# Another order of the parts, three small results on GpSimd, and a last tile in three groups of heads, in a hybrid attention and state-space layer

## The chip, the cores and the metric

One core of one Trainium2 chip runs the whole layer. The metric is device time in microseconds for one execution. Of three runs of the kernel before, the median was 692.42 us (692.40 to 692.64). The engines are TensorE (PE, with its weight loads as PEld), VectorE (DVE), ScalarE (ACT), GpSimd (POOL) and SyncE (SP), which here only issues transfers (DMAs). Each engine works through its own queue in order; semaphores make it wait for other engines and for transfers.

## What is computed

The input x has 1024 tokens of width 1024, in float32, one layer, one sequence. The reference, cut to what matters:

```python
mod = silu(c) @ w_ada + b_ada                       # shift, scale, gate
h = rms_norm(x, norm_g) * (1 + scale) + shift
q, kcr, vcr, ksl, vsl, kwn, vwn, z_a, g_br, u, z_s = split(h @ w_in)
kc, vc = rms_norm(compress(kcr)), compress(vcr)     # 63 blocks of 32 tokens
attn = g0 * softmax(q kc) vc + g1 * softmax(rq rk_slc, chosen blocks) v_slc
     + g2 * softmax(rq rk_win, last 512 tokens) v_win
attn = attn * silu(z_a)                             # 8 heads of 64, 2 key groups
y = gelu(s5(u)); y = y * sigmoid(y @ glu_w + glu_b) # complex diagonal recurrence
mix = concat(attn, y * silu(z_s)) @ w_out
return x + gate * mix
```

`s5` is a recurrence over the 1024 tokens with 32 groups of 16 channels and 64 complex states each.

## The kernel before, in words

The tokens are cut into 8 tiles of 128. The kernel keeps float32 accuracy by splitting an operand into a high and a low part (`hhi`, `hlo`; `wh`, `wl`; `oh`, `ol`) and adding three matmul products. High parts are casts on ACT, low parts a subtraction on DVE, on GpSimd, or an accumulating transfer.

The stages, in the order of time:

- x is loaded; its squares are summed (`sq`, in x_squares), the columns of `w_ada` are multiplied with silu(c) and summed (`wada`, in mod_chunk, a DVE product of 128x1024 for each 128 columns), and h is formed, transposed and split. A step named h`k``n` forms chunk k of half n.
- Projections of h go to keys and values (`kk`, normed, then `ropeb` is a rotary product and `kr` the rotated sum on GpSimd), to the S5 input (`U`), and to the raw keys and values of the compressed branch. A weight slice is loaded (`wr`, `wraw`), cast on ACT (`wh`, `wsp`) and its low part subtracted (`wl`, `wsp`).
- S5 runs in four scans of 8 groups each. For scan s, `prep` builds matrices from the parameters (tiles ta, tb, tc_, td, `s5W`, `s5CA`), `tables` the turning factors (`s5tab`), `mats` the kernel `Kt`, stored into `s5T` by eight transfers; `U` is stored to DRAM (`ud`) and loaded in another layout by eight transfers (`s5X`). Then `scan` takes `pvv` (PE), copies it to `zw` (four ACT copies), turns it with six DVE products (`z`, `zw`), scans it twice (tensor_tensor_scan) and turns it back; `out` computes `py` from `s5X` and the resulting `z`, copies it to `Y` and stores it (`yd`) through GpSimd's queue.
- Compressed keys, the gates z (pieces z0_0 to z7_7), and the GLU (`pglu`, `tg`, `zz` loaded again, `ps`) follow. The heads of the attention run through five steps: ha (scores `S`, row maxima `st`, exponentials `pp`), hs (reciprocals), hb and hc (weights `hl` in float16, transposed by transfers from SP into `PT`), ub (products `po`). While a score tile waits for its exponential, PE cannot fill it again.
- The output projection: `so` for the S5 half, `wo` for weights, `at` and `ao` for the attention half of a tile (unit_b, attn_trans, attn_out, out_half), with the last tile handled by last_out.

What sets the order is the table `ORD` (lines 27 to 56): names of parts, run in the order of the table, each of which adds its instructions to the queues; the framework's scheduler may then put an instruction behind one that is ready earlier on the same engine. `FLG` (line 57) says which engine does a small operation (d for DVE, p for GpSimd, a for ACT, t for an accumulating transfer). Nearly all transfers are issued by SP, in order: a store that waits for its data holds back every load behind it. The lines of the profile that the steps touch: 140 (dma), 148 (scalar_tensor_tensor) and 151 (tensor_tensor), which are helpers, 208 (cast of weights), 826 (`zw` copies), 853 (`py` from `z`), 1187 (row maxima), 1306 (out_half) and 1320 (last_out).

The part that releases the last tile:

```python
    def out_half(i, n, p):
        r = M["ps"][:, i, halves(n)]
        o = f2([128, 512], F32, "o")
        tt(dve, o[:], p[:], M["gate"][:, halves(n)], OP.mult)
        on = FLG.get(f"ao{i}{n}", "d")
        if on == "t":
            pool.dma_start(o[:], r, accum_op=OP.add)
        else:
            tt({"p": pool, "d": dve}[on], o[:], o[:], r, OP.add)
        dma(out.rearrange("(a p) d -> p a d", p=128)[:, i, halves(n)], o[:], "O")
```

Of the kernel before, what the change touches and what calls it, by code (L numbers as in the profile page):

```python
# [1619 lines left out]
```

## Time and profile before

| | |
|---|---|
| median of 3 runs | 692.42 us |
| the profiled execution | 691.38 us |
| its span, first to last instruction | 689.5 us |
| PE busy | 623.5 us, 90% |
| DVE busy | 567.3 us, 82% |
| ACT busy | 377.9 us, 55% |
| GpSimd busy | 148.6 us, 22% |
| mean granted clock of TensorE | 0.98 |
| mean DMA rate over the span | 169 GB/s |

The profiled execution is one run; its span lies 1.88 us under its own time, and its time 1.04 us under the median. Busy shares are means over stages that differ, so a stage is read from its own timeline: which engine stands still, until when, and what it was given at that moment. In a timeline, an entry with "x2" or more joins equal instructions that follow each other, and its duration is that of the group; the square brackets hold the idle time before it and what ended it.

### The profile page before, as it was taken

The page shows a single profiled execution, that of the slowest core. Times are in us where ns is not written, and L with a number is a line of the kernel's source. Part 1 is how long each engine was busy: PE and PEld are TensorE (multiplying, and loading weights), DVE is VectorE, ACT ScalarE, POOL GpSimd, SP SyncE. Part 2 cuts the span into 40 slices and gives each one's busy share as a digit, 9 for nine tenths or more (in the row PEclk, how much of TensorE's full clock was granted, in tenths as well). Part 3 has the DMA queues.
Part 4 walks back from the last instruction along what each step waited for, and adds up shares of the span by engine and source line. Part 5 has one row for each costly group of instructions (what it writes and reads, how often), then busy time and mean ns, then how long its engine had stood idle before and what let it go on. Part 6 is the DMA issues. An engine that isn't in the chain of part 4 may idle for free.

```text
span 689.5 us, 12618 instructions
## 1 busy us (share of the span) xinstructions
PE 623.5 (90%) x4662; PEld 492.1 (71%) x4662; DVE 567.3 (82%) x1106; ACT 377.9 (55%) x732; POOL 148.6 (22%) x159
## 2 busy tenths in 40 slices
PE   2478999999698999999999999989899999799996
PEld 0356787788587886888788887556677777687775
DVE  5998999777937889876677787998898998998872
ACT  3677413735162252555586786547756855756640
POOL 0153209147232020640011101132001220011010
PEclk9989999999899999999999999999999999999999
DMA  8975211355276624373656868499689599688994
GB/s 319 417 246 104 47 62 41 115 158 136 64 246 199 212 68 109 83 231 94 131 139 154 207 186 183 124 207 208 183 172 206 132 226 222 184 215 213 224 222 86
DMA packets 209759, 116.76 MB, mean 169 GB/s; under 512 B 159073, under 2 KB 188513, under 8 KB 209698
## 3 DMA queue, kind: packets, MB, share of 16 engines
q1 hardware_dynamic: 205858, 109.38, 61.5%
q0 software_dynamic: 3840, 6.57, 4.0%
q8 instruction: 37, 0.61, 0.3%
q14 instruction: 24, 0.20, 0.1%
HBM read 58.10 MB, written 18.61 MB: 111 GB/s over the span
## 4 chain that ended last, share of the span: by engine, by line
PE 41%; DVE 21%; issue 5%; ACT 4%; DMA 2%; SPq 1%; POOL 1%; DVEq 0%; ACTq 0%; POOLq 0%
PE pcp L351 9%; PE po L1053 8%; PE S L1170 7%; DVE hl L148 4%; PE po L1263 3%; PE pglu L1015 3%; DVE st L1187 3%; PE ptp L331 2%; PE ptp L332 2%; PE ptp L330 1%; DVE ps L151 1%; ACT pp L1203 1%; DVE z L151 1%; PE pg L530 1%; PE ph L901 1%
## 5 line engine op out<-in xcount | busy, mean ns | idle before, releaser
L1203 ACT ACTIVATE pp<-S,st 128x640 f32<-128x640 f32 (+7 forms) x128 | 88.6, 699 | 60.5 <-DVE st L1187 46.5
L148 DVE SCALAR_TENSOR_TENSOR hl<-pp,st,hl 128x640 f16<-128x640 f32 (+7 forms) x128 | 100.5, 817 | 4.9 <-ACT hl L1222 4.8
L1222 ACT ACTIVATE hl<-pp,st 128x640 f16<-128x640 f32 (+7 forms) x128 | 85.2, 728 | 8.2 <-DVE st L151 7.1
L1053 PE MATMUL po<-wo,oh 128*128 128x512 f32 x264 | 85.2, 407 | 3.7 <-DVE wo L151 2.4
L351 PE MATMUL pcp<-hhi,wh 128*128 128x512 f32 x208 | 84.8, 408 | 0.0
L351 PE MATMUL pcp<-hhi,wl 128*128 128x512 f32 x208 | 82.6, 397 | 0.0
L351 PE MATMUL pcp<-hlo,wh 128*128 128x512 f32 x208 | 82.4, 396 | 0.0
L1187 DVE TENSOR_REDUCE st<-S 128x1 f32<-128x1024 f32 (+3 forms) x64 | 57.5, 916 | 6.9 <-PE S L1170 6.7
L1170 PE MATMUL S<-kT,qh 128*128 128x128 f32 (+3 forms) x192 | 60.7, 375 | 1.0 <-ACT pp L1203 0.7
L1053 PEld LDWEIGHTS po<-wo,oh 128*128 128x128 f32 x264 | 48.7, 191 | 14.9 <-DVE wo L151 3.8
L330 PE MATMUL ptp<-wsp,hhi 128*128 128x512 f32 x128 | 53.5, 420 | 6.5 <-ACT hhi L296 4.1
L1263 PE MATMUL po<-V,PT 128*128 128x64 f16 x1584 | 59.0, 193 | 0.0
L1263 PEld LDWEIGHTS <-PT 128*128 128x128 f16 x1584 | 54.0, 98 | 5.7 <-issue 5.1
L1170 PE MATMUL S<-kT,ql 128*128 128x128 f32 (+3 forms) x192 | 55.3, 346 | 0.1
L332 PE MATMUL ptp<-wsp,hlo 128*128 128x512 f32 x128 | 53.0, 416 | 1.5 <-POOL hlo L151 1.5
L331 PE MATMUL ptp<-wsp,hhi 128*128 128x512 f32 x128 | 53.5, 418 | 0.5 <-DVE wsp L151 0.5
L151 POOL TENSOR_TENSOR qr<-ropeb 128x512 f32<-128x512 f32 x16 | 23.5, 1488 | 121.7 <-DVE ropeb L151 69.7
L1053 PE MATMUL po<-wo,ol 128*128 128x512 f32 x120 | 47.9, 402 | 0.8 <-DVE ol L151 0.8
L1170 PEld LDWEIGHTS S<-kT,qh 128*128 128x128 f32 x192 | 33.7, 193 | 17.2 <-issue 11.8
L351 PEld LDWEIGHTS pcp<-hlo,wh 128*128 128x128 f32 x208 | 39.1, 188 | 9.2
L351 PEld LDWEIGHTS pcp<-hhi,wh 128*128 128x128 f32 x208 | 39.2, 189 | 8.3
L351 PEld LDWEIGHTS pcp<-hhi,wl 128*128 128x128 f32 x208 | 39.2, 188 | 8.1
(327 smaller groups left out, 1351.5 us busy)
## 6 DMA issues: line engine op xcount, KB each, us to landing
wada<-in_w_adaT_dram SPq DMA_DIRECT2D x24, 512.0 KB, 6.6
wr<-in_w_in_dram SPq DMA_DIRECT2D x14, 512.0 KB, 4.5
x<-in_x_dram SPq DMA_DIRECT2D x8, 512.0 KB, 6.8
wor<-in_w_out_dram SPq DMA_DIRECT2D x8, 512.0 KB, 4.5
out_dram<-o SPq DMA_DIRECT2D x16, 256.0 KB, 2.5
wraw<-in_w_in_dram SPq DMA_DIRECT2D x15, 256.0 KB, 4.7
xo<-in_x_dram SPq DMA_DIRECT2D x14, 256.0 KB, 3.4
ud<-U SPq DMA_DIRECT2D x4, 512.0 KB, 3.2
```

The lines of the kernel that those rows point to most:

```text
L148: dve.scalar_tensor_tensor(out=o, in0=a, scalar=s, in1=b, op0=o0, op1=o1, **kw)
L151: e.tensor_tensor(out=o, in0=a, in1=b, op=op)
L330: pe.matmul(p, H(k)[:, tsl], w[:, 0, :], start=k == 0, stop=False)
L331: pe.matmul(p, H(k)[:, tsl], w[:, 1, :], start=False, stop=False)
L332: pe.matmul(p, H(k, True)[:, tsl], w[:, 0, :], start=False, stop=k == 7)
L351: pe.matmul(p[:], w[:, k, :], H(k, l)[:, halves(half)], start=(k == 0 and w is hi and not l), stop=(k == 7 and l))
L1053: pe.matmul(p, a[x][:, k, :], w[y][:, halves(n)], start=k == 0 and m == 0, stop=k == 3 and m == 2)
L1170: pe.matmul(R[:, c0:c1], w, x, start=bank not in opened, stop=False, skip_group_check=True)
L1187: dve.tensor_reduce(out=st[br], in_=us[br][0][:, :W], axis=AX.X, op=OP.max, negate=True)
L1203: act.activation(pp[:, :W], R[:, :W], AF.Exp, bias=st[br], accum_out=st4[:, 1, 2 * (h % 2) + br:2 * (h % 2) + br + 1])
L1222: act.activation(hl[:, :W], pp[:, :W], AF.Copy, scale=st[br])
L1263: pe.matmul(o, p, v, start=first, stop=end, skip_group_check=True)
```

## The change

A fifth of the names in `ORD` stand elsewhere, most of them by one to five places; two results move to another engine at the start (`sq2` from ACT to DVE, `h21` from DVE to GpSimd), and two adds of the output projection go from DVE to GpSimd (`ao21`, `ao40`). The last tile's attention heads 4 to 7, projected together before, are now projected as pairs: heads 4 and 5, then 6 and 7, and a new step `lo` (last_halves) ends the tile. The projection of one group is issued after the transposes (`pat`) of the next have been put behind it. A list `LATE`, empty here, has no effect. The number of matmuls is the same.

```diff
-sc1 sc0 lb pu xl_0 sq0 sq2 sq1 sq3 ma7 mb4 ma0 rstd0 mb0 kvaw0 ma5 xl_1 xsc0 sq5 xb10 sq4 xb00 sq6 sq7 mg mc0 h00 mb2
+sc1 sc0 xl_0 sq2 sq0 sq3 pu ma7 mb4 ma0 sq1 lb rstd0 mb0 ma5 kvaw0 xsc0 xl_1 xb00 sq5 xb10 sq4 sq6 sq7 mg mc0 h00 mb2
...
-cU3 mats1 kpat1 xl1 kvb7 kpb0 tq kpb1 kpbn0 u2 qaw0 u3 mod0 mod1 out0 prep2 tab1 cVC kpbn1 scan1 out1 tab2 xl2 cmpk
+cU3 mats1 xl1 kpat1 kvb7 kpb0 tq kpb1 kpbn0 u2 qaw0 u3 mod0 mod1 prep2 kpbn1 tab1 cVC out0 scan1 out1 tab2 xl2 cmpk
...
-    cw2456="d", cw512="d", cw640="d", h00="p", h01="d", h10="p", h11="t", h20="p", h21="d", h30="d", h31="d", h40="d",
+    cw2456="d", cw512="d", cw640="d", h00="p", h01="d", h10="p", h11="t", h20="p", h21="p", h30="d", h31="d", h40="d",
-    qw0="d", qw1="d", qw2="d", qw3="d", qw4="d", qw5="d", qw6="t", qw7="d", sq0="d", sq1="a", sq2="a", sq3="d",
+    qw0="d", qw1="d", qw2="d", qw3="d", qw4="d", qw5="d", qw6="t", qw7="d", sq0="d", sq1="a", sq2="d", sq3="d",
-    ao01="d", so1="d", at1="p", ao10="d", ao11="d", so2="p", at2="p", ao20="d", ao21="d", so3="d", at3="p", ao30="d",
+    ao01="d", so1="d", at1="p", ao10="d", ao11="d", so2="p", at2="p", ao20="d", ao21="p", so3="d", at3="p", ao30="d",
-    ao31="d", so4="d", ao40="d", ao41="d", so5="d", at5="p", ao50="d", ao51="d", so6="d", at6="p", ao60="d", ao61="d",
+    ao31="d", so4="d", ao40="p", ao41="d", so5="d", at5="p", ao50="d", ao51="d", so6="d", at6="p", ao60="d", ao61="d",
...
     def unit_b(i, h, br):
-        first = br == 0 and (j == 0 if last else h == 0)
+        first = br == 0 and (h in (0, 4, 6) if last else h == 0)
...
-        if br and j == 3 and (g or last):
+        if br and (h in (3, 5, 7) if last else h == 7):
...
-            hs = slice(4 * g if last else 0, 4 * g + 4)
+            hs = slice({3: 0, 5: 4, 7: 6}[h] if last else 0, h + 1)
...
-    def last_out(i, g):
-        if g == 0:
+    def last_out(i, hs):
+        if hs.start == 0:
...
+        else:
+            for n in range(2):
+                outproj(LO["p"][n][:], LO["a"], 0, n, LO["k"])
         za = LO["za"]
-        ks = (2 * g, 2 * g + 1)
-        kk = slice(2 * g, 2 * g + 2)
+        kk = slice(hs.start // 2, hs.stop // 2)
+        ks = range(kk.start, kk.stop)
+        w = 128 * len(ks)
...
         hi, lo = LO["a"]
         act.copy(hi[:, kk], za[:, kk])
         tt(dve, lo[:, kk], za[:, kk], f32(hi[:, kk]), OP.subtract)
+        LO["k"] = ks
+
+    def last_halves():
+        i = OB[-1]
         for n in range(2):
-            outproj(LO["p"][n][:], LO["a"], 0, n, ks)
-            if g:
-                out_half(i, n, LO["p"][n])
+            outproj(LO["p"][n][:], LO["a"], 0, n, LO["k"])
+            out_half(i, n, LO["p"][n])
```

What a few rows of the table do to the queues shows at three places. Lines of the changed file are one higher than before.

The first place is SP's queue between the stores of `U` for scans 2 and 3 and the X loads of scan 2. Before:

```order
68 L140 DMA ud_110<-U 128x1024
69 L140 DMA wraw<-in_w_in_dram 128x512
70 L140 DMA wada<-in_w_adaT_dram 128x1024
71 L140 DMA ud_111<-U 128x1024
72 L140 DMA wada<-in_w_adaT_dram 128x1024
73 L140 DMA wr_1560<-in_w_in_dram 128x8x128
74 L140 DMA s5X<-ud_110 16x8x128 x8
75 L140 DMA wraw<-in_w_in_dram 128x512 x2
```

and now:

```order
68 L141 DMA ud_110<-U 128x1024
69 L141 DMA wraw<-in_w_in_dram 128x512
70 L141 DMA s5X<-ud_110 16x8x128
71 L141 DMA ud_111<-U 128x1024
72 L141 DMA wada<-in_w_adaT_dram 128x1024 x2
73 L141 DMA s5X<-ud_110 16x8x128
74 L141 DMA wr_1539<-in_w_in_dram 128x8x128
75 L141 DMA s5X<-ud_110 16x8x128 x6
76 L141 DMA wraw<-in_w_in_dram 128x512 x2
```

Both `wada` loads now stand behind the second store of `U`, and ahead of `wr`; two of the eight X loads stand ahead of `wr` and six behind it.

The second place is DVE's queue between the `wada` products that go with those loads and scan 1, whose first instructions are the products that write `z`. Before:

```order
343 L151 TENSOR_TENSOR tc__1534<-s5P,s5c 128x512
344 L148 SCALAR_TENSOR_TENSOR wada,macc<-wada,sc 128x1024
345 L151 TENSOR_TENSOR td<-s5P,s5c 128x512
346 L151 TENSOR_TENSOR tb<-s5f,s5x 128x384
347 L151 TENSOR_TENSOR s5W<-tc__1534,td 128x512
348 L151 TENSOR_TENSOR s5tab<-ta,tb 128x4x96
349 L151 TENSOR_TENSOR wl_1559<-wr_1560,wh_1558 128x1024
350 L151 TENSOR_TENSOR ta<-s5f,s5x 128x384
351 L151 TENSOR_TENSOR tb<-s5f,s5x 128x384
352 L151 TENSOR_TENSOR ropeb<-kk,cs 128x512
353 L151 TENSOR_TENSOR s5tab<-ta,tb 128x4x96
354 L151 TENSOR_TENSOR ropeb<-kk,cs 128x512
```

and now:

```order
342 L152 TENSOR_TENSOR td<-s5P,s5c 128x512
343 L152 TENSOR_TENSOR tb<-s5f,s5x 128x384
344 L152 TENSOR_TENSOR s5W<-tc__1504,td 128x512
345 L816 MEMSET rho 128x4
346 L152 TENSOR_TENSOR ropeb<-kk,cs 128x512 x2
347 L149 SCALAR_TENSOR_TENSOR wada,macc<-wada,sc 128x1024
348 L152 TENSOR_TENSOR s5tab<-ta,tb 128x4x96
349 L149 SCALAR_TENSOR_TENSOR wada,macc<-wada,sc 128x1024
350 L152 TENSOR_TENSOR ta<-s5f,s5x 128x384
351 L152 TENSOR_TENSOR tb<-s5f,s5x 128x384
352 L149 SCALAR_TENSOR_TENSOR mod<-macc,bada 128x1 x2
353 L152 TENSOR_TENSOR s5tab<-ta,tb 128x4x96
```

The tc and td products, s5W and both ropeb stand ahead of the two `wada` products; before, td, tb and s5W stood behind the second one, and ropeb behind `wl`. The loads of `wada` are the ones above.

The third is the end of DVE's queue: the last tile. Before:

```order
940 L148 SCALAR_TENSOR_TENSOR za<-za,vsc,pat 128x256
941 L151 TENSOR_TENSOR oh<-za,oh 128x256
942 L148 SCALAR_TENSOR_TENSOR za<-za,vsc,pat 128x256
943 L151 TENSOR_TENSOR oh<-za,oh 128x256
944 L151 TENSOR_TENSOR o<-po,gate 128x512
945 L151 TENSOR_TENSOR o<-o,ps 128x512
946 L151 TENSOR_TENSOR o<-po,gate 128x512
947 L151 TENSOR_TENSOR o<-o,ps 128x512
```

and now:

```order
936 L149 SCALAR_TENSOR_TENSOR za<-za,vsc,pat 128x256
937 L152 TENSOR_TENSOR oh<-za,oh 128x256
938 L149 SCALAR_TENSOR_TENSOR za<-za,vsc,pat 128x128
939 L152 TENSOR_TENSOR oh<-za,oh 128x128
940 L149 SCALAR_TENSOR_TENSOR za<-za,vsc,pat 128x128
941 L152 TENSOR_TENSOR oh<-za,oh 128x128
942 L152 TENSOR_TENSOR o<-po,gate 128x512 x2
943 L152 TENSOR_TENSOR o<-o,ps 128x512
```

The second group of 256 columns became two of 128, and one of the two final adds is no longer here; it is the last operation of GpSimd's queue. In SP's queue ahead of scan 0, the store of the rotated keys (`kTd`) moved from behind the last seven X loads to in front of them. On GpSimd the two kr ahead of scan 1 now stand behind seven of the stores of `yd`.

## Rows read from the trace of the kernel before

**Rows 1.** The page, part 1: busy us, share of the span and instructions

```profile
PE 623.5 (90%) x4662; PEld 492.1 (71%) x4662; DVE 567.3 (82%) x1106; ACT 377.9 (55%) x732; POOL 148.6 (22%) x159
```

**Rows 2.** PE's waits: us in total, times, longest us

```profile
PE S L1170 <- ACT pp L1203: 10.6, 13, 3.3
PE py L853 <- DVE z L151: 6.2, 1, 6.2
...
PE ptp L330 <- ACT wsp L208: 2.4, 2, 1.9
...
PE pvv L824 <- DMA s5X<-ud: 1.2, 1, 1.2
...
PE pw L795 <- ACT Kt L785: 0.5, 1, 0.5
```

**Rows 3.** Timeline of PE; start, us, line, op, [idle before <-releaser]

```profile
184.93 0.80 PE L853 MATMUL py<-z,s5CA 128*128 128x127 f32 x2 [6.19 <-DVE z L151]
```

**Rows 4.** Timeline of DVE, 154 to 186 us

```profile
161.98 2.03 DVE L148 SCALAR_TENSOR_TENSOR wada<-wada,sc 128x1024 f32<-128x1024 f32 x1 [4.09 <-DMA wada<-in_w_adaT_dram]
...
171.94 2.37 DVE L151 TENSOR_TENSOR z<-zw,s5tab 128x512 f32<-128x512 f32 x2
174.24 1.78 DVE L151 TENSOR_TENSOR zw<-zw,s5tab 128x512 f32<-128x512 f32 x1
```

**Rows 5.** Timeline of ACT, 148 to 187 us

```profile
164.46 1.05 ACT L208 CAST wh<-wr 128x1024 fp32r<-128x1024 f32 x1 [7.61 <-DMA s5X<-ud]
...
165.93 2.38 ACT L826 COPY zw<-pvv 64x512 f32<-64x512 f32 x4
168.34 0.41 ACT L763 COPY s5tab<-s5f 128x256 f32<-128x256 f32 x1
```

**Rows 6.** Timeline of SP, 148 to 187 us: DMA issues

```profile
156.66 0.33 SPq L140 DMA_DIRECT2D ud<-U  x1
157.04 0.43 SPq L140 DMA_DIRECT2D wada<-in_w_adaT_dram  x1
157.58 0.66 SPq L140 DMA_DIRECT2D wr<-in_w_in_dram  x1
```

**Rows 7.** The tile wr, 140 to 175 us: landing of its one load

```profile
DMA to landing us min/median/max: 6.7/6.7/6.7
```

**Rows 8.** Timeline of DVE, 104 to 134 us: start of scan 0

```profile
126.75 1.30 DVE L151 TENSOR_TENSOR z<-zw,s5tab 128x512 f32<-128x512 f32 x2 [4.30 <-ACT zw L826]
127.97 0.68 DVE L151 TENSOR_TENSOR zw<-zw,s5tab 128x512 f32<-128x512 f32 x1
```

**Rows 9.** Timeline of GpSimd (POOL), 154 to 186 us

```profile
153.76 2.37 POOL L140 DMA_DIRECT2D yd<-Y  x4
...
172.02 3.46 POOL L151 TENSOR_TENSOR kr<-ropeb 128x512 f32<-128x512 f32 x2 [4.48 <-DVE mod L148]
```

**Rows 10.** Two us: busy time of PE, PEld, DVE, ACT, POOL; PEclk, DMA, GB/s

```profile
186.00:188.00 2.00, 2.00 (x11) 2.00 (x11) 1.97 (x6) 0.00 (x0) 0.00 (x0) 0.51 0.51 134
```

**Rows 11.** Timeline of DVE, 8 to 26 us

```profile
16.91 1.11 DVE L148 SCALAR_TENSOR_TENSOR rstd<-rsq,rstd 128x4 f32<-128x4 f32 x1
```

**Rows 12.** Timeline of GpSimd, 8 to 26 us

```profile
16.74 1.27 POOL L151 TENSOR_TENSOR wsp<-wraw,wsp 128x512 fp32r<-128x512 f32 x1 [15.54 <-ACT wsp L208]
```

**Rows 13.** Timeline of SP, 104 to 134 us

```profile
117.06 3.43 SPq L140 DMA_DIRECT2D s5X<-ud  x7
120.59 0.61 SPq L140 DMA_DIRECT2D kTd<-kh  x1
```

**Rows 14.** Timeline of DVE, 452 to 474 us

```profile
459.90 2.06 DVE L151 TENSOR_TENSOR ps<-tg,zz 128x512 f32<-128x512 f32 x1 [0.26 <-DMA zz<-zsd]
461.80 1.84 DVE L148 SCALAR_TENSOR_TENSOR hl<-pp,st,hl 128x640 f16<-128x640 f32 x1
```

**Rows 15.** Timeline of PE, 452 to 474 us

```profile
466.73 0.22 PE L1170 MATMUL S<-dmask,identb 128*128 128x128 bf16 x1 [3.27 <-ACT pp L1203]
```

**Rows 16.** Timeline of DVE, from 679 us to the end

```profile
685.72 0.69 DVE L151 TENSOR_TENSOR o<-o,ps 128x512 f32<-128x512 f32 x1
```

More of the change, by code (lines that the diff above doesn't have):

```diff
@@ new lines @@
+h20 xb21 h30 kvaw3 xb11 h11 h21 xb31 kvaw6 xb40 mc5 h31 ma4 s5l mc4 ll h40 xb70 mc7 h70 xb50 u0m ma6 h50 kva0 kva1
+xb51 kva2 u1m xb61 u2m u3m xb60 mc6 h51 h61 xb71 xb41 h60 kva3 tb h41 kva4 kvaw7 h71 s5p kva5 kva6 sw u4m u5m kva7 u6m
+u7m tabf kpa0 kpa1 kvb0 cKC kpan0 kvb1 kvb2 prep0 kvb3 kvb4 kvb5 u0 cU2 mats0 kpat0 tab0 kvb6 xl0 prep1 scan0 kpan1 u1
+cU3 mats1 xl1 kpat1 kvb7 kpb0 tq kpb1 kpbn0 u2 qaw0 u3 mod0 mod1 prep2 kpbn1 tab1 cVC out0 scan1 out1 tab2 xl2 cmpk
+qaw1 cmpv kpbt0 qaw2 mod2 mod3 mod4 mats2 hidk qaw3 qaw4 qaw5 qa0 qa1 qa2 kpbt1 qa3 mod5 qa4 qa5 qaw6 mod6 qaw7 qa6
@@ new lines @@
+qw2 ct1 ha12 ha13 z3_3 qr2 ub04 ub05 ha14 hs13 ub06 ha15 z3_4 z3_5 cz5 ub07 z3_6 z3_7 hs15 z4_0 hb12 hb13 ub10 hb14
+hb15 qt20 ub11 ha16 ha17 hc12 hc13 hc14 yp02 z4_1 z4_2 hs17 qt21 hb16 ub12 ha20 ha21 hb17 z4_3 ca2 hc15 hs21 ha22 z4_4
+z4_5 ha23 hc16 z4_6 z4_7 hb20 ub13 cz6 hb21 hc17 hs23 hc20 yp03 yp10 ub14 z5_0 z5_1 z5_2 hb22 z5_3 z5_4 ub15 qw3 qr3
+z5_5 hc21 cz7 z5_6 ha24 hb23 ha25 ub16 ub17 hs25 hb24 z6_0 z5_7 hc22 hc23 hc24 ha26 ha27 ct2 hs27 qt30 z6_1 z6_2 z6_3
+z6_4 z6_5 z6_6 yp11 z6_7 yp12 hb25 hb26 hc25 ha30 ha31 qt31 ha32 ha33 hs31 hs33 ca3 hb27 z7_0 hb30 ub20 hc26 hb31 z7_1
@@ new lines @@
+glul z7_2 z7_3 hb32 z7_4 hc27 z7_5 hc30 hc31 hc32 ha34 yp13 ub21 qw7 hb33 ha35 hs35 z7_6 z7_7 hc33 ct3 sp glu00 grow
+ha36 ha37 glu03 qr7 qt70 glu01 hb34 hc34 qt71 ha70 ub22 ub23 ub24 hb35 ha71 ub25 hc35 ca7 ub26 ub27 hs37 hb36 hc36
+ub30 hb37 ct7 glu11 glu02 glu12 glu10 hs71 hb70 qw6 qr6 ha72 ub31 ub32 ub33 hc37 hc70 at0 ha73 hs73 glu13 wo10 wo11
+hb71 hc71 hb72 hc72 ha74 hb73 wo12 wo13 ub34 ub35 ub36 ha75 qt60 hc73 ub37 hs75 hb74 hb75 ub70 ha76 ha77 hs77 ub71 so0
+so1 qt61 hc74 hc75 hb76 hb77 ca6 ub72 hc76 hc77 ha60 ha61 ub73 hs61 hb60 ub74 hc60 ct6 qw5 hb61 ha62 ha63 so2 hs63 qr5
@@ new lines @@
+hb62 ub75 ha64 hc61 hc62 hb63 ha65 ub76 hs65 so4 hb64 hb65 ha66 ha67 ub77 ca5 ub60 ub61 hc63 hc64 so5 qt50 ub62 ha50
+qt51 hs67 hb66 hb67 hc65 qw4 qr4 ub63 so7 hc66 ha51 hc67 hs51 ub64 hb50 hb51 hc50 hc51 so6 ha52 ha53 ha54 ha55 ha56
+ub65 hs53 hb52 hb53 ub66 so3 wo00 wo01 wo02 wo03 ct5 hc52 qt41 at3 hc53 ub67 ub50 hs55 hb54 hb55 hc54 ha57 hs57 ca4
+ao30 hc55 ao31 ao00 ao01 qt40 hb56 hb57 at1 at2 ao10 ha40 ha41 hs41 hb40 hc56 hb41 hc57 hc40 ha42 ub51 ao11 ha43 ub52
+ao20 hs43 hb42 ct4 hb43 hc41 hc42 ao21 ha44 ha45 hc43 ub53 hs45 ub54 at7 ao70 hb44 hb45 ub55 ao71 ha46 ub56 ub57 ub40
@@ L56 @@
+at5 at6 ha47 ao50 ao51 ao61 hc44 hs47 ub41 hc45 hb46 hc46 hb47 ao60 ub42 ub43 ub44 ub45 ub46 hc47 ub47 lo
 """.split()
@@ L70 @@
 SMB = 11
+LATE = []
 OA, OB = [0, 1, 2, 3], [7, 6, 5, 4]
@@ L1534, in hymba @@
     it.pop(f"at{OB[-1]}")
+    I("lo", f"ub{OB[-1]}7")(last_halves)
     for n in range(2):
```

42 lines of the change are left out of this document (11 added, 31 removed).

## The prediction

> **What bounds the kernel.** I read the busy table first. TensorE (PE) works 623.5 us of a span of 689.5 us [rows 1], and the change issues the same matmuls. So the time moves only by PE's idle time, some 66 us, or by matmuls that run at another clock. Next I read PE's waits. Three of them lie where the diff moves instructions: 6.2 us for VectorE's (DVE's) z before the first `py<-z` of scan 1, 10.6 us in 13 pieces for the exponentials that free the score tiles, and 1.2 us for the X transfer of scan 0 [rows 2]. Then I followed each wait back on the engine it names.
>
> The 6.19 us at 184.93 [rows 3] end when scan 1 ends on DVE. Its first z starts at 171.94; ahead of it DVE waited 4.09 us in its queue for a `wada` transfer (to 161.98), and the `wada` product that follows took 2.03 us [rows 4]. ScalarE (ACT) waited 7.61 us, to 164.46, then cast `wh`, and only then copied pvv into zw (from 165.93) and wrote s5tab (168.34) [rows 5]: the wait is booked to an X transfer, but the cast reads `wr`, issued at 157.58 [rows 6], which needs 6.7 us to land [rows 7], so at 164.3. Within the scan the first two z took 2.37 us and the next zw 1.78 us [rows 4], against 1.30 and 0.68 us in scan 0 [rows 8]. GpSimd's two kr ran beside them, 172.02 to 175.48 [rows 9].
>
> The clock is the last view: while PE waits it falls to half, 0.51 from 186 to 188 us [rows 10], so PE's first work after the wait, 184.93 to about 188, is done at 1.2 GHz.
>
> **The scan 1 stage (the main term).** On DVE the change puts both ropeb and the tc, td, s5W work before the `wada` products, so the 4.09 us wait is filled. On GpSimd kr now follows the first seven yd stores. GpSimd's four yd stores took 2.37 us [rows 9], so seven take about 4.1 us; the Y copies can end near 159 (U ends just before the ud store at 156.66 [rows 6]), the stores near 163, two kr of 1.73 us (half of 3.46) near 166.5. That is ahead of the scan, which then costs its clean durations. It ran from 171.94 to 184.93, 12.99 us; less 2.37 − 1.30 and 1.78 − 0.68, together 2.17 us, it takes 10.8 us.
>
> On the other side stands SyncE's (SP's) queue: both `wada` loads are now issued ahead of `wr`, with one X load. One more 512 KB goes in front of `wr`. The nearest rows give its price: the `wada` issued at 157.04 was used at 161.98, and `wr`, issued 0.54 us later, landed 2.3 us after that [rows 4, 6, 7]. So `wr` lands between 164.3 (six of the eight X loads now lie behind it) and 168.5 (the price twice); I take 167.2, the price once and 0.6 us for issues. From the landing ACT needs the cast (1.05), four zw copies (2.38) and s5tab (0.41) [rows 5]: z can start at about 171.0, and DVE's wl, 2.3 us behind the landing, is done before. The start gains 0.9 us (bounds −0.4 and 3.8, by the two ends of the landing), the scan 2.2: **−3.1 us** at the first `py`. The chain behind it (Y, yd, G copies, pk, s5T) keeps its order, and DVE and ACT shift with PE. Some is lost where a transfer's landing ends a wait that isn't released by this chain: PE waits 2.4 us in all for wsp casts of freshly loaded `wraw` [rows 2]. Between 0 and 1.9 us of the gain could be eaten there; I take 0.6. If the wait shrinks to about 3 us, PE's clock probably still falls; I count nothing there.
>
> What the Trainium skill would make of the kr overlap: its page "SBUF — State Buffer", section "SBUF: two separate sides", says that the ports that DVE and GpSimd share are locked for a whole instruction and the loser blocks fully. By that, moving kr away would free two whole GpSimd operations, 2 × 1.27 = 2.5 us instead of 2.17. The trace agrees for one small operation: a DVE rstd that began at 16.91 ended when GpSimd's wsp did, 1.11 us later [rows 11, 12].
>
> **The X transfer of scan 0.** SP now issues the 512 KB kTd store before the seven X loads instead of after them; before, the loads took 3.43 us to issue from 117.06 and the store 0.61 us from 120.59 [rows 13]. So the last X load is issued 0.61 us later, and lands between 0.6 and 1.9 us later (its transfer queued behind 512 KB, bounded by the 2.3 us price above less what drains in the 3.4 us of issuing). Against it, pk and pw go earlier on PE and save the 0.5 us wait for Kt [rows 2]. Net **+0.5 us** (−0.5 to +1.4).
>
> **The GLU stage.** PE waits 3.27 us at 466.73 for a score tile [rows 15]. Ahead of its row maxima DVE ran ps 2.06 us and the 640-wide hl 1.84 us [rows 14], both beside GpSimd's qr, which starts when ropeb ends. If qr doubled both, as kr nearly doubled z, 1.95 us of them are the overlap. The change puts hl ahead of ropeb, hence ahead of qr, and splits the two ropeb around ps, so qr now falls on tg and the maxima instead. Between 0 and 2 us are saved; I take **−0.5 us**, since the same qr still runs somewhere and since the later score waits, of which there are twelve, can take up what one gives back.
>
> **The tail.** The last tile's final heads are projected as pairs. Before, DVE did four `o` operations in a row, the last of them from 685.72, 0.69 us long, to 686.41 [rows 16]. Now the pat of the last pair stands behind six matmuls of the pair before (half of 3.08 us for twelve), so the first product starts about when it did, four times 0.7 us before that end, at 683.6; the second follows at once, and the add of the first half runs on GpSimd, 1.27 us clean [rows 12], ending near 685.6, when DVE's last add does. That is **−0.3 us** (−0.7 to +0.2). The lock on that page of the Trainium skill speaks against such a division of work: by it DVE's add would wait for GpSimd's and end near 686.3, a gain of 0.1 us.
>
> **The rest.** At the start the `sq` of one tile goes from ACT to DVE: 1.2 us on DVE in front of the `wada` products, beside waits for x that are longer; DVE's first rstd comes about 0.4 us later, and what ends PE's first wait is a `wada` landing later on. h21's subtraction and the add of tile 2 go to GpSimd, 1.27 us instead of 0.68, under PE work. The many swaps of z pieces and head stages between 255 and 660 us lie under a PE that is nearly full. I count nothing for these, with ±0.8 us.
>
> **Sum.** −3.1 + 0.6 + 0.5 − 0.5 − 0.3 = −2.8 us against the profiled execution, 691.38 us (span 689.5 and 1.88 us outside it): 688.6. The median of the runs, 692.42, stands 1.04 us above that execution, so the forecast is **689.6 us**.
>
> **The rivals.** (1) *The loads eat it, and X is late: slower.* If `wr` lands at 171 or later, z starts at 174.8, and even a clean scan ends at 185.6, 0.7 us after the old one. From a landing of 170.3 on, the stage loses. With X of scan 0 1.4 us late and nothing elsewhere that is 692.42 + 0.7 + 1.4 = 694.5 us. For it: ACT really stood for `wr` in the queue, and one more load is put ahead. Against: six X loads move behind it, and 170.3 asks for six microseconds more than now, where one load cost 2.3. Chance 0.11. (2) *The change doesn't do what it says:* z starts when it did since s5tab or `wr` is just as late, and the scan saves its 2.17 us, of which the wraw landings eat most; 0.5 us come back from X. Time 692.42 − 2.2 + 1.9 + 0.5 − 0.8 = 691.8. Chance 0.26. (3) *Everything carries and the clock holds:* with nothing lost behind scan 1, X at no cost and the full 2 us of the GLU stage the sum is −3.1 − 2.0 − 0.3 = −5.4; 687.0 us, and 1.5 us less if the 3.1 us of half-clock work [rows 3, 10] run at 2.4 GHz. Chance 0.15. (4) *The three operations moved to GpSimd hold DVE up:* each saves DVE 0.68 us (a clean operation of that size, [rows 8]) and can block it for 1.27 us [rows 12], so up to 1.8 us are lost in all: 691.4 us. That is what the lock on the page of the Trainium skill would make of them. The trace bears it out for one operation [rows 11, 12], but two of the three have PE work over them. Chance 0.08.
>
> **How the numbers follow.** My forecast has 0.40. 0.2% or 1.4 us is about what a measurement of this kernel can tell from none. Forecast and rival 3 lie below 691.04; of rival 2 and 4 a fifth does: faster 0.62. Same 0.27, which is the rest of these. Slower 0.11. The range leaves out half of rival 3's end and most of rival 1: **687.0 to 693.0 us**.
>
> **What would show it.** Right: the wait of the first `py<-z` falls from 6.19 to about 3 us, the first two z take 1.3 us, kr stands before 168 us, and `wr` lands by 168. Wrong: z's start at 172 or later, an X wait of 2 us or more at 122, wider waits for wsp near 214, or a 466 us wait that stays at 3.3 us. If the waits shrink and the end does not come earlier, a later transfer took the gain.

## The result, and the profile after

The changed kernel takes 688.02 us (median of 6 runs, 686.86 to 689.40), against 692.83 us for the kernel before on the same chip (6 runs). The ratio is 0.991, with a 95% interval of 0.9889 to 0.993: faster by 0.7% to 1.1%. The profiled execution took 687.92 us, 3.46 us less than the profiled one before. The forecast was 689.6 us. The direction and the range held; the gain was larger than forecast, and most of it came from another place. Line numbers after the change are one higher than before.

The page, part 1, of the kernel after answers to [rows 1]:

```profile
PE 622.1 (91%) x4662; PEld 492.2 (72%) x4662; DVE 570.0 (83%) x1107; ACT 377.1 (55%) x732; POOL 152.5 (22%) x162
```

TensorE (PE) issues the same 4662 matmuls and is even busy 1.4 us less: some ran at a higher clock. Its waits after (us in total, times, longest) answer to [rows 2]:

```profile
PE S L1171 <- ACT pp L1204: 8.5, 13, 1.9
...
PE pkt L480 <- POOL kr L152: 2.9, 1, 2.9
...
PE py L854 <- DVE z L152: 2.4, 1, 2.4
```

The wait for z fell from 6.2 to 2.4 us, as forecast. That is not the gain: PE came to this wait 4.7 us later than before (at 183.43 instead of 178.74), 2.05 of it from ahead of scan 0 and 1.8 in new waits for zw (0.86) and G (0.97). The score waits fell by 2.1 us, their longest from 3.3 to 1.9. A wait for kr is new.

To see where the time went, I matched the PE instructions of the two traces and took the median of (start after minus start before). This offset grows where time is lost and falls where it is gained:

| at (us, before) | 80–100 | 120–160 | 190–210 | 230 | 450 | 470 | 490 | 520 | 650 | whole execution |
|---|---|---|---|---|---|---|---|---|---|---|
| after − before | +1.2 | +2.05 | +1.12 | +2.2 | +2.97 | −0.22 | −1.30 | −2.60 | −2.96 | −3.46 |

The first column is partly the new order itself: run 3 below, without the new wait for kr, has 1.6 there and 0.3 at 120. So up to 450 us the changed kernel is 3 us late, scan 1 gives back only 0.9 of it, and the GLU stage between 460 and 520 us makes up 5.6 us.

**A new wait ahead of scan 0.** Timeline of PE after, at the three places that matter:

```profile
107.67 0.66 PE L480 MATMUL pkt<-ident,kr 128*128 128x128 f32 x4 [2.89 <-POOL kr L152]
...
185.79 0.49 PE L854 MATMUL py<-z,s5CA 128*128 128x127 f32 x2 [2.36 <-DVE z L152]
...
468.16 0.22 PE L1171 MATMUL S<-dmask,identb 128*128 128x128 bf16 x1 [1.74 <-ACT pp L1204]
```

The change put `kpat0`, PE's transposes of the rotated keys, ahead of `kvb6` and `xl0`. GpSimd's kr was hardly earlier than before (it began at 103.70, first row of the next fence, against 104.00), so PE, which takes its instructions in order, stood still until it ended.

**Scan 1.** Timeline of GpSimd after:

```profile
103.70 3.91 POOL L152 TENSOR_TENSOR kr<-ropeb 128x512 f32<-128x512 f32 x2 [19.67 <-DVE ropeb L152]
...
165.33 1.42 POOL L152 TENSOR_TENSOR s5CA<-ta,tb 128x512 f32<-128x512 f32 x1
166.69 4.29 POOL L141 DMA_DIRECT2D yd<-Y  x7
171.00 2.52 POOL L152 TENSOR_TENSOR kr<-ropeb 128x512 f32<-128x512 f32 x2
```

and of VectorE (DVE), which answers to [rows 4]:

```profile
164.36 1.23 DVE L149 SCALAR_TENSOR_TENSOR wada<-wada,sc 128x1024 f32<-128x1024 f32 x1 [1.83 <-DMA wada<-in_w_adaT_dram]
...
165.51 1.65 DVE L152 TENSOR_TENSOR s5tab<-ta,tb 128x384 f32<-128x384 f32 x1
...
168.70 1.67 DVE L152 TENSOR_TENSOR tb<-s5f,s5x 128x384 f32<-128x384 f32 x1
170.29 2.08 DVE L149 SCALAR_TENSOR_TENSOR mod<-macc,bada 128x1 f32<-128x1 f32 x2
172.30 1.64 DVE L152 TENSOR_TENSOR s5tab<-ta,tb 128x384 f32<-128x384 f32 x1
...
175.00 1.28 DVE L152 TENSOR_TENSOR z<-zw,s5tab 128x512 f32<-128x512 f32 x2
176.20 0.68 DVE L152 TENSOR_TENSOR zw<-zw,s5tab 128x512 f32<-128x512 f32 x1
```

z and zw are clean, as forecast, and the scan is 10.8 us long (175.00 to 185.79), as worked out. But no brackets stand behind z: DVE went without a gap from the `wada` landing at 164.36 to 175.00, 10.64 us. Four of its groups were stretched beside GpSimd: clean ones of the same size took 0.55 (s5tab), 0.54 (tb) and 0.14 us (one mod) before, so 1.10 + 1.13 + 1.80 + 1.10 = 5.1 us were lost here. The two mod write one element per partition and took 2.08 us; the first of them alone took 2.01 and ended at 172.30, with the first kr (171.00 plus half of 2.52). The Trainium skill states on its page "SBUF — State Buffer", section "SBUF: two separate sides", that one engine's instruction holds the shared ports to its end, and these two ends agree with that. Why the mod, whose turn came 0.6 us before kr began, did not go first is not shown. The mod and the last s5tab, 2.9 of the 5.1 us, lie beside kr, which had only moved from beside z to beside the operations ahead of z; the first s5tab lies beside s5CA. The tb lies beside yd issues alone, beside which the z of run 12 took their clean time, so its stretch stays unexplained.

The 5.1 us are not all new. Before, three operations of this row were stretched beside GpSimd as well:

```profile
163.94 1.54 DVE L151 TENSOR_TENSOR td<-s5P,s5c 128x512 f32<-128x512 f32 x1
165.40 1.65 DVE L151 TENSOR_TENSOR tb<-s5f,s5x 128x384 f32<-128x384 f32 x1
```

With the `wada` product ahead of them (2.03 us in [rows 4], 1.23 above) that is 0.8 + 0.9 + 1.1 = 2.8 us. From the `wada` landing to z the row took 9.96 us before (161.98 to 171.94) and 10.64 now: without the stretches it would have shrunk from 7.2 to 5.5 us, and the stretch grew by 2.4.

SyncE (SP) and the landing of `wr` answer to [rows 6, 7], ScalarE (ACT) to [rows 5]:

```profile
159.10 1.19 SPq L141 DMA_DIRECT2D wada<-in_w_adaT_dram  x2
...
160.89 0.43 SPq L141 DMA_DIRECT2D wr<-in_w_in_dram  x1
```

```profile
DMA to landing us min/median/max: 8.8/8.8/8.8
```

```profile
169.68 1.06 ACT L209 CAST wh<-wr 128x1024 fp32r<-128x1024 f32 x1 [9.25 <-DMA wr<-in_w_in_dram]
...
173.04 0.41 ACT L764 COPY s5tab<-s5f 128x256 f32<-128x256 f32 x1
```

`wr` landed at 169.7; less the 2.05 us by which everything is late there, that is 167.6, and I had said 167.2. ACT was done at 173.45, and z began 1.55 us later, because DVE was not.

**The GLU stage.** Windows of before (columns as in [rows 10]), then of after:

```profile
468.00:470.00 2.00, 2.00 (x6) 1.23 (x7) 1.76 (x2) 1.03 (x2) 1.27 (x1) 0.50 0.92 270
470.00:472.00 2.00, 2.00 (x5) 0.86 (x3) 0.60 (x3) 2.00 (x5) 0.00 (x0) 0.68 1.01 378
...
486.00:488.00 2.00, 2.00 (x7) 1.56 (x6) 0.79 (x1) 2.00 (x3) 0.00 (x0) 0.50 0.96 217
```

```profile
470.00:472.00 2.00, 2.00 (x8) 1.02 (x7) 1.47 (x2) 1.47 (x4) 1.27 (x1) 1.00 1.30 238
...
486.00:488.00 2.00, 2.00 (x13) 1.58 (x12) 1.49 (x2) 2.00 (x3) 0.00 (x0) 1.00 1.14 237
```

Before, PE stood for 3.27 us [rows 15] and then worked at 1.2 GHz (granted clock 0.50) for some 3 us, and again after the next score wait near 486. After, the wait is 1.74 us and the clock stays at 1.00. The eight `pglu` matmuls behind the wait took 4.69 us before and 3.65 after. The timeline of DVE shows why the wait is shorter; before:

```profile
464.17 1.94 DVE L1187 TENSOR_REDUCE st<-S 128x1 f32<-128x1024 f32 x2
```

and after:

```profile
458.63 2.06 DVE L149 SCALAR_TENSOR_TENSOR hl<-pp,st,hl 128x1024 f16<-128x1024 f32 x2
...
465.60 1.94 DVE L1188 TENSOR_REDUCE st<-S 128x1 f32<-128x1024 f32 x2
```

Before, the row maxima `st` began 0.7 us after PE had run out of work (466.73 − 3.27 = 463.46). Now they begin 0.8 us ahead of that (468.16 − 1.74 = 466.42), since the large hl run earlier in DVE's queue; before, one of them and the stretched ps stood right in front of the maxima [rows 14]. The 5.6 us are 1.5 for this wait, 1.6 for the work behind it at full clock (offset +1.43 to −0.21 across it), 1.1 around the next score wait and the work behind it (to −1.30 at 490), and 1.3 up to 520, in which a 0.95 us wait of `pqc` is gone.

The full clock is not secured by this order. Run 6 below has the same order here, and PE's wait and the window behind it read:

```profile
465.28 0.22 PE L1171 MATMUL S<-dmask,identb 128*128 128x128 bf16 x1 [2.03 <-ACT pp L1204]
466.00:468.00 2.00, 2.00 (x10) 1.46 (x8) 1.92 (x3) 0.62 (x2) 0.54 (x1) 0.53 1.49 194
```

By the same offsets, from 450 to 530 us, the new order of this stage gave 5.6 us in the changed kernel, 5.9 in run 3, 6.0 in run 7 and 5.9 in run 8, but 2.8 in run 6, 2.9 in run 9, 4.1 in run 10 and 4.1 in run 12. In runs 6, 9 and 10 the clock fell behind this wait (2.03, 1.83 and 2.05 us long); in run 12 the wait itself was 3.07 us.

**The tail.** From PE's end of the last head (`ub47`) to DVE's last add it took 6.45 us before (679.96 to 686.41) and takes 5.93 now (676.79 to 682.72). The last rows of DVE and of GpSimd, against [rows 16]:

```profile
681.56 1.16 DVE L152 TENSOR_TENSOR o<-o,ps 128x512 f32<-128x512 f32 x1
```

```profile
680.91 1.26 POOL L152 TENSOR_TENSOR o<-o,ps 128x512 f32<-128x512 f32 x1 [20.83 <-DVE o L152]
```

DVE's add, 0.69 us alone, took 1.16 beside GpSimd's.

### The profile page after: what moved, and what is told of

Same layout as the page of the kernel before. It is cut to its first block, busy times and chain, and to the rows that moved or that the text cites. A ratio compares the mean times of both kernels' runs of the same rounds, so it can differ in the third digit from the quotient of the medians.

```text
span 685.9 us, 12622 instructions
## 1 busy us (share of the span) xinstructions
PE 622.1 (91%) x4662; PEld 492.2 (72%) x4662; DVE 570.0 (83%) x1107; ACT 377.1 (55%) x732; POOL 152.5 (22%) x162
## 4 chain that ended last, share of the span: by engine, by line
PE 45%; DVE 32%; DMA 8%; ACT 6%; issue 6%; POOL 1%; SPq 1%; DVEq 0%; ACTq 0%; POOLq 0%
PE pcp L352 14%; PE po L1054 8%; PE S L1171 7%; DVE hl L149 5%; DMA wada<-in_w_adaT_dram 3%; PE po L1264 3%; DVE st L1188 3%; PE pglu L1016 3%; DVE z L152 2%; DVE wada L149 1%; PE ptp L333 1%; DVE ps L152 1%; PE ptp L332 1%; ACT pp L1204 1%; PE ptp L331 1%
## 5 line engine op out<-in xcount | busy, mean ns | idle before, releaser
L1171 PE MATMUL S<-kT,ql 128*128 128x128 f32 (+3 forms) x192 | 53.8, 339 | 0.1
```

The lines of the kernel that those rows point to most:

```text
L1171: pe.matmul(R[:, c0:c1], w, x, start=bank not in opened, stop=False, skip_group_check=True)
```

## The experiments

Single runs of one kernel lie up to 9.6 us apart (the kernel before: 688.0 to 697.6 us in 29 runs of one chip), so each experiment is read twice: by its ratio to the kernel before on the same chip, and, for a place, by offsets between matched instructions of two traces. A trace is one execution, and an offset scatters too: run 1 has the program of the kernel before up to 450 us, and its offset to it wanders there between −0.8 and +1.6 us. A reading of 1 us at one place therefore counts only together with a wait that explains it, or when several traces agree. The question after the result was whether the order in the GLU stage gives the gain by itself, or whether other parts do and that stage only takes back what came late.

**1. Before, with only the new GLU stage.** The 79 names of `ORD` from `hb33` to `hb75`, in the changed kernel's order:

```diff
-hb33 yp13 ub21 qw7 ha35 hs35 z7_6 z7_7 sp hc33 ct3 glu00 grow ha36 ha37 glu03 qr7 qt70 hb34 hc34 glu01 qt71 ha70 ub22
+yp13 ub21 qw7 hb33 ha35 hs35 z7_6 z7_7 hc33 ct3 sp glu00 grow ha36 ha37 glu03 qr7 qt70 glu01 hb34 hc34 qt71 ha70 ub22
...
```

> The kernel before, with the changed order of the GLU stage alone (78 names of the table, from hb33 to ub71, some 435 to 505 us). Theory A, the gain is made in the GLU stage by a shorter wait for a score tile and by matmuls that stay at full clock: 5.2 us less than before, about 687.3 us, with the wait near 467 us at 1.8 us or less and the clock at 1.00 from 468 to 472 us. Theory B, the gain is made at scan 1, as forecast, and the later stage only receives it: within 1 us of before, and the wait near 467 us still 3 us.

689.32 us (12 runs), ratio 0.9945 (0.9917 to 0.9973). In its trace the offset to before falls by 4.3 us in this stage, the score wait is 1.58 us at 465.89, and the granted clock is 1.00 from 466 to 476; behind the next score wait, 1.89 us at 482.96, it fell to 0.50. The stage's order gives the larger part of the gain by itself (the expectation had 687.3 us).

**2. After, with the old GLU stage.** The reverse exchange.

> The changed kernel, with the old order of the same 78 names. Theory A: the stretch up to 430 us costs 2.9 us and the tail and the last heads give 1.2 us, so this runs 1 to 2 us slower than before, about 694 us. Theory B: it keeps most of the gain, about 689 us.

690.98 us (12 runs), ratio 0.9977 (0.9946 to 1.0008): nothing that can be told from no change is left; some 694 us had been expected. Its score waits come to 12.8 us, the longest 3.5, and the clock is 0.50 from 470 to 476. Without this stage the rest of the change is worth nothing that these runs can show.

**3. After, with the old order of tile 0's keys.**

```diff
-mats0 kpat0 tab0 kvb6 xl0
+kvb6 mats0 xl0 kpat0 tab0
```

> The changed kernel, with the old order of five names alone (kvb6 mats0 xl0 kpat0 tab0), so that the key transposes stand behind the last projection matmuls again. Theory A, the new PE wait of 2.9 us for GpSimd's kr at 107.7 us and the half clock behind it cost 2.1 us that reach the end: 2 us less than the changed kernel, about 686 us, and no wait over 1 us between 104 and 110 us. Rival: the 2 us come back at a later wait (scan 1 or the w slices near 215 us) and the time is that of the changed kernel within 0.6 us.

685.47 us (6 runs), ratio 0.9893 (0.9851 to 0.9935). PE's wait for kr is gone, and the offset to the changed kernel is −1.75 us from 120 us on and −2.35 from 230. In these two traces this part of the change cost 1.7 to 2.4 us. The ratios alone don't tell the two kernels apart: 0.9893 and 0.991 lie in each other's intervals.

**4. Before, with only the new order around scan 1.**

```diff
-out0 prep2 tab1 cVC kpbn1
+prep2 kpbn1 tab1 cVC out0
```

> The kernel before, with the changed order of five names alone (prep2 kpbn1 tab1 cVC out0, ahead of scan 1). Theory A: the scan itself loses the overlap with kr and takes 10.8 us instead of 13.0, but its first product starts 1 us later, behind wr and the two wada products; the first py comes 1 to 1.5 us earlier, and the end moves by under 1.5 us. Theory B, the forecast: z starts 0.9 us earlier, py 3.1 us earlier, the time falls by 2.5 to 3 us.

691.51 us (12 runs), ratio 0.9976 (0.9951 to 1.0001). z is clean (1.28 us) but starts at 173.10, 1.2 us later than in [rows 4], and the wait for z falls to 2.37 us at 183.90, 1.03 us earlier. The part is worth 1 us here, a third of what I gave it, and by the ratio it can't be told from nothing. PE also has a new wait of 2.43 us for ScalarE's G, with the work between it and z, so that the smaller z wait overstates the gain.

**5. Before, with more work for PE in the wait.** The four transposes `pat` in front of the 3.27 us score wait are done five times:

```diff
-        for k in range(4):
+        for k in list(range(4)) * (5 if i == 0 else 1):
```

> The kernel before with the four transposes of tile 0 near 463 us done five times over (16 more matmuls of 128 columns, about 2.5 us, in the 3.27 us in which PE waits); the result stays the same. Theory A, half of the GLU gain is the clock that falls after that wait: PE idles under 1 us there, the clock stays at 1.00 from 468 to 472 us, and the time falls by 1.0 to 1.6 us. Rival: the clock follows something else (it is 0.5 at 468 us all the same), and the time stays within 0.4 us of before.

693.45 us (12 runs), ratio 1.0008 (0.997 to 1.0047). The median says nothing, but the place does; its PE timeline and windows:

```profile
469.26 2.38 PE L1296 MATMUL pat<-ident,A 128*128 128x128 f32 x20
473.09 0.22 PE L1170 MATMUL S<-dmask,identb 128*128 128x128 bf16 x1 [1.45 <-ACT pp L1203]
```

```profile
474.00:476.00 2.00, 2.00 (x11) 1.28 (x10) 1.68 (x3) 0.96 (x2) 1.22 (x1) 1.00 0.93 282
476.00:478.00 2.00, 2.00 (x6) 0.82 (x5) 0.59 (x3) 2.00 (x5) 0.04 (x1) 1.00 1.01 384
```

The same results arrive at the same point of DVE's queue, and 16 needless transposes fill 1.75 us (2.38 against 0.63 for four) of the wait. The clock then stays at 1.00, and the offset falls by 1.7 us across it (+6.44 to +4.72). This separates the two effects, in one execution: the fall of the clock behind this wait cost 1.7 us by itself. With the old order of this stage and no filler the clock fell here each time that it was read (waits of 3.27 us before, 3.20 in run 4, 3.52 in run 2).

**6. After, with the last add of `ao40` on VectorE again.** `ao40="p"` becomes `"d"`.

> The changed kernel with the last tile's first add on DVE again. From the end of the last head's products (ub) to the end of the last add: 5.9 us in the changed kernel. Four operations of 0.69 us in a row from the same first product give 6.1 us, so the add on GpSimd is worth 0.2 us; if the three groups alone had made the tail shorter, it stays at 5.9 us; if they gave nothing, it is 6.4 us as before.

A single run, 687.54 us. From the end of `ub47` to the last add it is 5.94 us, against 5.93: the add on GpSimd is worth nothing. The whole 0.5 us of the tail are there without it. The first product of the last tile comes 3.36 us behind `ub47` instead of 3.64, and the four operations, now two products and then two adds, take 2.58 instead of 2.81. Both go with the three groups of heads; they were not tried apart.

**7. Run 3, with the old order around scan 1 as well.**

> The changed kernel with the old order of the keys (as in the run before it) and, besides, the old order of the five names ahead of scan 1. Theory A: 0.7 to 1.5 us slower than with the old order of the keys alone, some 686.5 us, with the 6 us wait of the first py back. Theory B: 3 us slower, some 688.5 us.

686.77 us (6 runs), ratio 0.9906 (0.9869 to 0.9943). Against run 3 the offset rises by 0.9 us at 190: the same worth as in run 4, seen from the other side. The wait for z is 5.28 us again. At 342 us this trace lost another 4.3 us against run 3 in a part that both have alike: a score wait took 2.60 instead of 1.12 us, and the clock stood at 0.50 behind it from 342 to 348.

**8. Run 3, with `mod0` and `mod1` (the `wada` products and their loads) behind `kpbt0`.** The two names leave their place behind `u3`.

> The changed kernel with the old order of the keys, and with mod0 and mod1 (the two wada loads and products ahead of scan 1) moved behind kpbt0, past scan 1. Theory A, what holds scan 1's start is DVE's row from the landing of wada on, each operation of which is stretched by GpSimd, and wr queued behind two wada loads: wr lands 2 to 4 us earlier, the first z starts 3 us earlier (about 170 us), PE's wait for the first py falls from 2.4 to under 0.5 us, the clock stays at 1.00 from 184 to 188 us, and the time falls by 1.5 to 3.5 us against the old order of the keys alone, to about 683 us. Rival: the five wada products that now stand together at 197 to 208 us hold up Kt there, and the time is the same or up to 3 us longer.

682.52 us (6 runs, 681.71 to 683.20), ratio 0.9841 (0.9803 to 0.988), the fastest of all. `wr` is issued at 158.44 and lands 4.7 us later. DVE and PE:

```profile
166.17 2.94 DVE L152 TENSOR_TENSOR z<-zw,s5tab 128x512 f32<-128x512 f32 x2 [0.45 <-ACT zw L827]
169.04 1.78 DVE L152 TENSOR_TENSOR zw<-zw,s5tab 128x512 f32<-128x512 f32 x1
```

```profile
179.77 0.80 PE L854 MATMUL py<-z,s5CA 128*128 128x127 f32 x2 [2.99 <-DVE z L152]
```

z starts 7.1 us earlier than in run 3 (173.23), although kr stretches it again (at 166.82 on GpSimd). The expected wait of under 0.5 us did not come; it grew from 2.38 to 2.99, and the clock fell to 0.50 behind it. py is 4.3 us earlier, of which 1.9 us are left at the end; PE's next wait for a `wsp` cast takes 3.26 us at 214 instead of 1.35.

**9. Run 8, with `mod0` to `mod4` behind `qaw5`.**

> Old order of tile 0's keys as before, and the modulation products mod0 to mod4 all moved behind qaw5. If what was gained by moving mod0 and mod1 (682.5 us) came from the earlier wr store in front of scan 1 alone, mod2 to mod4, which stood behind scan 1 already, add nothing: z again near 166.2, first wait of TensorE for z near 3.0 us, 682 to 683.2 us. If the modulation products also hold up TensorE behind the scan (by what they read from the weights' queue), the offset falls by another 1 us or more between 200 and 230: 681.5 us or less.

697.62 us (12 runs), ratio 1.0065 (1.0029 to 1.0101): 15 us slower than run 8, and neither expectation saw it. SP, GpSimd and PE:

```profile
207.70 10.96 SPq L141 DMA_DIRECT2D wada<-in_w_adaT_dram  x6
```

```profile
220.16 0.59 POOL L214 DMA_DIRECT2D wsp<-in_w_in_dram  x1 [16.58 <-issue]
```

```profile
223.24 1.22 PE L331 MATMUL ptp<-wsp,hhi 128*128 128x512 f32 x2 [3.18 <-DMA wsp<-in_w_in_dram]
...
230.42 0.79 PE L332 MATMUL ptp<-wsp,hhi 128*128 128x512 f32 x1 [5.97 <-DMA wsp<-in_w_in_dram]
```

Scan 1 is unchanged. But six `wada` loads of 512 KB now go out together from 207.70, and GpSimd issues two weight loads at 220.16 and 224.27 that it issued at 208.56 and 218.10 in run 8. PE waits 9.2 us for them. Of the rest of the loss, some 3 us arise in the GLU stage, where the clock fell behind a score wait of 1.83 us; the remainder was not traced. Why GpSimd came to the two loads so late the trace does not name, and no run tested it.

**10. Run 9, with `kpbn1` (kr) behind scan 1 as well.**

> The kernel with mod0 to mod4 behind qaw5, and kpbn1 (kr on GpSimd) moved behind tab2. If GpSimd's kr beside the scan is what stretches z from 1.3 to 2.9 us and zw to 1.8, z and zw are short again with kr behind them, TensorE's first wait for z falls by 1.5 us or more, and the time to 681 us or less. If kr only changes its place, TensorE waits for it at pkt of tile 1 (2 us or more, a wait that is not there now) and the time is 682.5 us or more.

698.97 us (9 runs), ratio 1.0088 (1.0054 to 1.0123). The weights' waits are those of run 9 (3.09 and 6.55 us). On DVE z takes 1.90 and zw 0.68 us, but the first scan instruction behind them takes 3.65 instead of 1.22, from 170.50, beside kr at 170.54: the stretch goes along with kr. PE's wait for z is no shorter (3.1 us), and neither expected time came.

**11. Before, with only eighteen names around `glu01` in the new order.**

```diff
-hb34 hc34 glu01 qt71 ha70 ub22 ub23 ub24 ub25 hb35 hc35 ub26 hs37 ub27 hb36 hc36 ca7 ha71
+glu01 hb34 hc34 qt71 ha70 ub22 ub23 ub24 hb35 ha71 ub25 hc35 ca7 ub26 ub27 hs37 hb36 hc36
```

> The kernel before with only some twenty names around glu01 to ct7 in the changed kernel's order: it changes on VectorE the order of the row maxima (st), the two large hl and the products ropeb, and little else. If VectorE's order in front of the softmax is what shortens TensorE's wait for S, the wait falls from 3.3 to about 1.6 us, TensorE's granted clock stays at 1.00 from 468 to 472, and the time is 688.5 to 690 us. If the gain hangs on the whole block (TensorE's own order and the transposes beside it), the wait stays at 3 us or more, the clock falls to .5 there, and the time is 691.5 to 693 us.

689.50 us (12 runs), ratio 0.9968 (0.994 to 0.9997). PE, and one window:

```profile
464.43 0.22 PE L1170 MATMUL S<-dmask,identb 128*128 128x128 bf16 x1 [1.81 <-ACT pp L1203]
...
466.30 3.65 PE L1015 MATMUL pglu<-y,glw 128*128 128x512 f32 x8
```

```profile
470.00:472.00 2.00, 2.00 (x24) 1.62 (x23) 1.86 (x3) 1.97 (x4) 0.00 (x0) 1.00 1.00 402
```

The offset falls by 3.4 us in the stage (−0.84 to −4.2), three quarters of what the 79 names of run 1 gave (there the clock fell behind the second score wait, here it did not). What these names do is mainly to let DVE have its row maxima early and its hl and ropeb in the new order; they also move some of PE's products, and that share was not tried apart.

**12. Run 8, with the two kr in front of scan 1 on VectorE.** `rope` takes the engine as an argument, and only this call gets VectorE.

```diff
-            tt(pool, o[:, :, :, 32 * h:32 * h + 32], two(c, h), two(b, 1 - h), op)
+            tt(e or pool, o[:, :, :, 32 * h:32 * h + 32], two(c, h), two(b, 1 - h), op)
```

> The kernel of 682.5 us (old order of tile 0's keys, mod0 and mod1 behind kpbt0), with only the two kr sums in front of scan 1 moved from GpSimd to VectorE, where one takes about 0.7 us instead of GpSimd's 1.7 and stands ahead of s5tab. If it is GpSimd's kr beside them that stretches VectorE's z and zw, they are back at 1.3 and 0.68 us (2.7 us saved for 0.9 to 1.4 us of kr ahead of them), z starts at about 167, TensorE's first wait for z falls from 3.0 to about 1.2 us, and the time to 680 to 681.5 us. If the stretch comes from something else (transfers, ScalarE's copies), z stays at 2.9 and zw at 1.8 us, all of the scan comes 0.9 us later, and the time is 683 to 684.5 us.

682.92 us (6 runs), ratio 0.987 (0.9824 to 0.9917). DVE, one window, and PE:

```profile
159.23 3.24 DVE L152 TENSOR_TENSOR kr<-ropeb 128x512 f32<-128x512 f32 x2
...
167.61 1.29 DVE L152 TENSOR_TENSOR z<-zw,s5tab 128x512 f32<-128x512 f32 x2
168.82 0.69 DVE L152 TENSOR_TENSOR zw<-zw,s5tab 128x512 f32<-128x512 f32 x1
```

```profile
180.00:182.00 2.00, 2.00 (x19) 1.95 (x18) 1.86 (x6) 0.75 (x2) 0.74 (x2) 1.00 0.62 164
```

```profile
178.41 0.49 PE L854 MATMUL py<-z,s5CA 128*128 128x127 f32 x2 [2.25 <-DVE z L152]
...
210.56 0.73 PE L331 MATMUL ptp<-wsp,hhi 128*128 128x512 f32 x2 [3.73 <-ACT wsp L209]
...
462.61 0.22 PE L1171 MATMUL S<-dmask,identb 128*128 128x128 bf16 x1 [3.07 <-ACT pp L1204]
```

That GpSimd's kr is what stretches z is now shown: without it z and zw save 2.74 us, for 1.44 us that z starts later. The time is not better for it: 680 to 681.5 us had been expected. PE's wait falls to 2.25 us, not to 1.2. The clock holds behind the wait, and the offset to run 8 falls by 3.5 us at 190. None of it reached the end: 1.2 us go in a wait for a `wsp` cast at 210, and 1.6 us in the score wait at 462, which is 3.07 us again in this timing (run 8: 1.44).

## Why the prediction was right and wrong

- **Direction and tail: right, the direction by luck.** The main term gave a third of its size or less, and most of the gain came from a term that I had at 0.5 us. The tail gave 0.5 us where 0.3 were taken, inside its bounds, with the three groups (run 6). By its own times (686.41 to 685.6) that term should have read 0.8, and it hung on the add on GpSimd, which gave nothing: DVE's last add was stretched beside it and ended 0.55 us behind it.
- **"The scan 1 stage (the main term)", −3.1 us: the size is wrong; it gave 0.9 to 1.1** (the table, runs 4 and 7). The scan's own 2.2 us came as worked out, and so did the landing of `wr` (its upper bound, "the price twice", is 168.9 by the rows and not 168.5). What failed is the step "z can start at about 171.0, and DVE's wl ... is done before". I followed the chain from `wr` over ACT, but in [rows 4] z has no brackets either: already before, ACT was done at 168.75 and DVE's queue set z's start. It had to be added up along DVE, from the `wada` landing on. There the change took out td, a tb, s5W and ropeb, and put in a second `wada` product, and GpSimd's s5CA and kr now stand beside these operations (5.1 us of stretch, 2.4 more than before): less the lateness of 2.05 us, z began 1.0 us later than before instead of 0.9 earlier. My GpSimd timeline, with kr ending near 166.5, was 7 us early (5 without that lateness): its queue was still at s5CA at 165. `out0`, whose stores the yd are, had moved behind `prep2` in the table, so on GpSimd they came behind the work of `prep2` (to s5CA, which ended at 166.75) and kr behind them; that work I had not put into the timeline. That z would start no earlier was rival 2; at this place it is what happened.
- **"The X transfer of scan 0", +0.5 us: right in sign, wrong in place.** The loss was 1.75 us or more (by the trace of run 3) and no transfer: I looked at SP's queue and saw that `pk` and `pw` went earlier on PE, but not that `pkt`, moved with them, asks for kr, which GpSimd had no earlier than before.
- **"The GLU stage", −0.5 us: the term that failed most; it gave 5.6** (run 1: 4.3; run 11: 3.4; 2.8 to 6.0 in the other traces with this order). I bounded it by the overlap with qr (0 to 2 us). But the hl moved ahead bring the maxima forward whatever qr does, 1.5 us at the wait. And I left out the clock, as if it mattered only at scan 1: the work behind the wait ran at 1.2 GHz before, and run 5 prices that alone at 1.7 us. That it ran at 2.4 GHz after is part luck, since in runs 6, 9 and 10 it did not. The view for it, the windows behind 466 us, I had not read. Rival 3, "the clock holds", stood at 687.0 us and came nearest, but by its mechanism at scan 1 it was as wrong as the forecast.
- **The rest.** Between 200 and 450 us 1.8 us were lost. Some 0.6 to 1.0 of that may go with the keys' order (run 3's distance to the changed kernel grows from 1.75 to 2.35 at 230 and 2.75 at 450); the rest was not traced, and is within the scatter of such offsets. One piece is a wait of 0.82 us at 227.53 for a weight load. Rival 4 (the operations moved to GpSimd) shows nothing at `ao40`; the other two were not tried apart.

The errors had opposite signs: the scan 1 stage gave about 2 us less than its term, the keys cost over 1 us more, 1.8 us went between 200 and 450, and the GLU stage gave 5 us more. That the total was only 1.6 us off (688.0 against 689.6) is luck.

## What to carry to other kernels

An operation that starts without idle time ahead of it is bound by its own engine's queue: add up that queue, with the stretched durations beside the other engine, instead of following the latest transfer. For every instruction moved forward on an in-order engine, look up when its operand was ready in the old trace: `kpat0` cost about 2 us that way, by the trace in which its move was taken back. And price a wait with the work behind it at the clock that the rows show there: shortening one by 1.5 us was worth 3.2 where the clock held (a wait of 1.74 instead of 3.27 us, and 1.6 us at full clock behind it), and less where it did not (run 6).
